# Four gate tiles leave the filling of the attention rounds and become two more Winograd column pairs

## The chip, the cores and the metric

One NeuronCore of a Trainium2 chip runs the whole program. The metric is the device time of one execution in microseconds (us). TensorE does the matrix products (PE in the profile; PEld its weight loads), VectorE is DVE, ScalarE ACT, GpSimd POOL, and SyncE (SP) issues nearly all DMAs.

## The reference

One decoder block over a sequence of 1024 tokens with width 1024, all float32, reduced here to the parts that the change touches:

```python
h = rms_norm(x, ln1_g)
proj = h @ w_in + b_in                  # 1024 x 6400
rq, rk, rv, rg, aq, ak, av, gate_a, gate_b = jnp.split(proj, SPLIT_IDX, axis=-1)
ry = head_group_norm(retention_chunkwise(rotary(rq), rotary(rk), rv), ret_norm_g)
branch_a = (silu(rg) * ry) @ w_ret_out
ay = sliding_window_sink_attention(rotary(aq), rotary(ak), av, attn_sinks)   # 16 heads of 64, window 128
branch_b = ay @ w_attn_out
merged = sigmoid(gate_a) * branch_a + sigmoid(gate_b) * branch_b             # both gates: 1024 columns of proj
x = x + merged @ w_out
x = x + (silu(h2 @ w_gate) * (h2 @ w_up)) @ w_down                           # h2 = rms_norm(x, ln2_g)
out = rms_norm(x, lnf_g)
```

gate_a and gate_b together are 2048 columns of the projection, 16 tiles of 128 columns, numbered 0 to 15 here (0 to 7 are gate_a).

## The kernel before

Every float32 operand of a product is split into a high and a low part (ScalarE casts the high part, VectorE subtracts to get the low one), and a product is three matmuls: high by high, high by low, low by high. A matmul has 128 rows of weights and streams 512 columns.

**Two ways to a column of the projection.** A *direct* tile of 128 columns costs 2 halves of the sequence x 8 blocks of the contraction x 3 = 48 matmuls (`mm_g`, lines 172 to 182). A *column pair* of 256 columns goes through a Winograd scheme of seven products P1 to P7 over half-size blocks, each 4 x 3 = 12 matmuls, so 84 for what costs 96 directly (`wproduct`, line 1018); for it POOL and DVE make sums of blocks. Before, eleven column pairs hold retention's q, k and swish gate and the gate tiles 0 to 5; the tiles 6 to 15 are direct.

**The attention stage.** It works through 32 units, one for a query block of 128 tokens (8 of them) and a quad of heads (4). A loop over i makes rounds, and in round i three units are at work. In the order of the program: the probabilities of unit i-2 are transposed on PE (`u_transpose`, L616), cast by ACT (L618), their low part taken by DVE (L619) and masked (L624); the scores of unit i are made on PE (`u_scores`, L581); ACT exponentiates unit i-1 (L604), and DVE normalises it (L607, L608); ACT and DVE copy out the scores of unit i and take their minimum (L590, L591, L593; L596 where the unit is the first of its quad); then comes the *filling*, and last the value products of unit i-2 on PE (`u_values`, L635). There is one pair of PSUM banks for scores, so the scores of unit i+1 wait until L591 has read those of unit i. The block is recorded under `in_order`: each of the five engines takes its instructions in just this order.

**The filling** is a list of items, run in steps of three matmuls: the projections of the q quads 1 to 3 (32 steps each, with rotary rotation behind them) and the direct gate tiles (16 steps each). Quad 0 and 20 steps are done ahead of round 0. `early` and `late` say how many steps the first `turn` rounds and the rest take. `prep` (L451 and L452 for a quad, L472 and L473 for a gate tile) splits the weights of the next item, from a slab of 512 KB which `load` has fetched into one of two buffers; the next loads (L442, L467) can start when both engines have read the old ones.

**The rotation** of half a quad is three tasks, one a round, at the end of the round's work on DVE: three operations (L514), three more, and two low parts (L533) after two casts on ACT (L530). The third also has SP store four tiles of 256 KB to `q_d` (L521); a round later SP reads them back in the layout for the scores (L526). The evicted halves (L492) use three rotating buffers of the tag `rab`, and the two `st` tiles have one buffer each, so an eviction or a first task waits for stores that still read the old tile.

After the filling come the products for retention's v (L861, DVE prepares sums of blocks for them), then the column pairs, the branch products, the output projection and the feed-forward part.

Of the kernel before, what the change touches and what calls it, by code (L numbers as in the profile page):

```python
# [20 lines left out]
NB = S // P  # L21
# [10 lines left out]
C_RQ, C_RK, C_RV, C_RG, C_AQ, C_AK, C_AV, C_GA, C_GB = (  # L32
    0, 512, 1024, 2048, 3072, 4096, 4224, 4352, 5376)
# [7 lines left out]
def hybrid_block(ctx: ExitStack, tc: tile.TileContext, x, ln1_g, w_in, b_in, ret_norm_g, w_ret_out,  # L41
# [74 lines left out]
    @contextmanager  # L116
    def in_order(*engines):

        traced = nc.cur_bb.bb.instructions
        last = traced[-1]  # L120
        yield
        start = next(k for k in reversed(range(len(traced))) if traced[k] is last) + 1
        prev = {}
        for i in traced[start:]:
            if i.engine in engines:
                if i.engine in prev:
                    tc.add_manual_dep(i, prev[i.engine],
                                      mybir.DependencyInfo(mybir.DependencyClass.NoSync, mybir.DependencyReason.DATA),
                                      reason="in_order")
                prev[i.engine] = i.name  # L130
# [194 lines left out]
    with tc.tile_pool(name="gt", bufs=1, side="right") as gt, tc.tile_pool(name="w1", bufs=1) as w1:  # L325
# [242 lines left out]
        def u_sink(u):  # L568
            g, b, nk, Bt, jb, qc = geo(u)
            scs[u] = (w1.tile([P, 4, 132], F32, tag="sc", bufs=3, name=f"sc{g}{b}"),  # L570
                      tiny.tile([P, 4], F32, tag="nm", name=f"nm{g}{b}"), tiny.tile([P, 4], F32, tag="den", name=f"den{g}{b}"))
            nc.gpsimd.tensor_copy(scs[u][0][:, :, P:P + 1], nsink[:, 4 * g:4 * g + 4].rearrange("p (j o) -> p j o", o=1))

        def u_scores(u):
            g, b, nk, Bt, jb, qc = geo(u)
            kv = g // 2
            k0 = (b - 1) * P if b > 0 else 0
            pt = sps[u] = spool[1].tile([P, 4, 2 * P], F32, tag="s4", name=f"s{g}{b}")
            for j in range(4):
                for z in range(2):  # L580
                    nc.tensor.matmul(pt[:, j, 0:nk], Bt[:, jb + j, qc], kst[:, kv, z, k0:k0 + nk], start=(z == 0),  # L581
                                     stop=(z == 1))

        def u_min(u):
            g, b, nk, Bt, jb, qc = geo(u)
            mk = amask[:, 0:P]
            pt = sps.pop(u)
            sc, nm, den = scs[u]
            if b > 0:
                nc.scalar.copy(sc[:, :, 0:P], pt[:, :, P:2 * P])  # L590
                nc.vector.copy_predicated(sc[:, :, 0:P], mk.bitcast(U32).rearrange("p (o s) -> p o s", o=1)  # L591
                                          .to_broadcast([P, 4, P]), pt[:, :, 0:P])
                nc.vector.tensor_reduce(out=nm, in_=sc[:, :, 0:P + 1], op=ALU.min, axis=mybir.AxisListType.X)  # L593
                return
            for j in range(4):
                nc.vector.tensor_tensor_reduce(out=sc[:, j, 0:P], in0=pt[:, j, 0:P], in1=mk, scale=1.0,  # L596
                                               scalar=nsink[:, 4 * g + j:4 * g + j + 1], op0=ALU.add, op1=ALU.min,
                                               accum_out=nm[:, j:j + 1])

        def u_exp(u):  # L600
            g, b, nk, Bt, jb, qc = geo(u)
            sc, nm, den = scs[u]
            for j in range(4):
                nc.scalar.activation(sc[:, j, 0:P + 1], sc[:, j, 0:P + 1], AF.Exp, scale=-1.0, bias=nm[:, j:j + 1],  # L604
                                     accum_out=den[:, j:j + 1])
            rd = tiny.tile([P, 4], F32, tag="rd", name=f"rd{g}{b}")
            nc.vector.reciprocal(rd, den)  # L607
            nc.vector.tensor_tensor(out=sc[:, :, 0:P], in0=sc[:, :, 0:P],  # L608
                                    in1=rd.rearrange("p (j o) -> p j o", o=1).to_broadcast([P, 4, P]), op=ALU.mult)

        def u_transpose(u):
            g, b, nk, Bt, jb, qc = geo(u)
            sc = scs.pop(u)[0]
            pt = ps("t", 2, f"pT{g}{b}")
            for j in range(4):
                nc.tensor.transpose(pt[:, j * P:(j + 1) * P], sc[:, j, 0:P], ident)  # L616
            p = w1.tile([P, 2, 512], F32R, tag="p", bufs=1, name=f"p{g}{b}")
            tie(acts, nc.scalar.copy(p[:, 0], pt))  # L618
            tie(vecs, nc.vector.tensor_tensor(out=p[:, 1], in0=pt, in1=f32(p[:, 0]), op=ALU.subtract))  # L619
            phs[u] = [(vev[:, b // 2], p)]  # L620
            if b > 0:
                mk = amask[:, P:2 * P].rearrange("p (o s) -> p o s", o=1).to_broadcast([P, 8, P])
                q = w1.tile([P, 2, 512], F32R, tag="q", bufs=1, name=f"q{g}{b}")
                nc.vector.scalar_tensor_tensor(out=q.rearrange("p z (j q) -> p (z j) q", j=4), in0=mk,  # L624
                                               scalar=float(b % 2 - 1), op0=ALU.add,
                                               in1=f32(p).rearrange("p z (j q) -> p (z j) q", j=4), op1=ALU.mult)
                phs[u].append((vdf[:, b - 1], q))
# [19 lines left out]
                nc.sync.dma_start(tb_d[n, :, half * 512:half * 512 + 512], t)  # L647
                yield

        order = list(range(6, 16))  # L650
        items = [QuadQ(0), QuadQ(1)] + [Gate(n) for n in order[0:2]] + [QuadQ(2)] + [Gate(n) for n in order[2:4]]
        items += [QuadQ(3)] + [Gate(n) for n in order[4:]]
        loaded = [0, 0]

        asked = [it for it in items for _ in range(it.raws)]
# [12 lines left out]
        def filling(n):  # L668
            it = items[n]
            while len(it.w) < it.size:  # L670
                prep(it)
            at = 23 if it.size == 2 else 4 if n + 1 < len(items) and items[n + 1].size == 2 else 0
            for k, _ in enumerate(it.products()):
                if k == at and n + 1 < len(items):
                    prep(items[n + 1])
                yield
# [6 lines left out]
        fl = Fill([filling(n) for n in range(1, len(items))])  # L683
        NU = 4 * NB
        fl.step(20)
        early, late, turn = 140, 68, 21
        with in_order(nc.tensor.engine, nc.sync.engine, nc.scalar.engine, nc.vector.engine, nc.gpsimd.engine):
            u_sink(0)
            for i in range(NU + 2):
                if i % NB == 0 and 0 < i < NU:  # L690
                    fl.until((1, 4, 7)[i // NB - 1])
                if i > 1:
                    u_transpose(i - 2)
                if i < NU:
                    u_scores(i)
                if 0 < i <= NU:
                    u_exp(i - 1)
                if i < NU:
                    u_min(i)
                while reads:  # L700
                    reads.pop(0)()
                on_act, on_dve, on_sp = task()
                do(on_act)
                if i + 1 < NU:
                    u_sink(i + 1)
                n, i0, m = (early, 0, turn) if i < turn else (late, turn, NU + 2 - turn)
                fl.step((i - i0 + 1) * n // m - (i - i0) * n // m)
                do(on_dve)
                do(on_sp)
                if i > 1:  # L710
                    u_values(i - 2)
                if 2 * NB + 4 <= i < 3 * NB + 4 and i % 2 == 0:
                    if i == 2 * NB + 4:
                        wv = act.tile([P, 16, 512], F32, tag="B", name="wv")
                    for q in ((1, 3, 0, 2)[i // 2 - NB - 2],):
                        nc.sync.dma_start(wv[:, 4 * q:4 * q + 4, :],
                                          w_in[(q // 2) * 512:(q // 2) * 512 + 512, C_RV + (q % 2) * 512:
                                               C_RV + (q % 2) * 512 + 512].rearrange("(k p) n -> p k n", p=P))
                if 3 * NB < i < NU and i % 2:

                    k = (i - 3 * NB) // 2
                    nc.vector.tensor_tensor(out=wv[:, 4 + k, :], in0=wv[:, 12 + k, :], in1=wv[:, 4 + k, :],
                                            op=ALU.subtract)
            fl.rest()
# [46 lines left out]
        return [kq.tile([P] + shape, F32, tag=t, name=f"{name}{t}") for t in ("kT", "qT")]  # L771

    cols = [c for h in range(RH) for c in ((C_RK, C_RQ, C_RK + 256, C_RQ + 256)[h], C_RG + 256 * h)]
    cols += [C_GA + 256, C_GA + 512, C_GA]
    NW = len(cols)

    with tc.tile_pool(name="rvp", bufs=1) as rvp:
# [528 lines left out]
    fl = Fill([bb_g(n) for n in range(8)])  # L1306
# [51 lines left out]
    with tc.tile_pool(name="w3", bufs=1) as w3:  # L1358
# [52 lines left out]
        late = in_order(nc.vector.engine, nc.scalar.engine)  # L1411
# [448 lines left out]
    early, kept = [], []  # L1860
# [268 lines left out]
```

## Time and profile before

| | |
|---|---|
| median of 3 runs | 1550.93 us (1550.89 to 1553.74) |
| profiled execution | 1553.45 us, span 1551.7 us, granted clock 0.997 |
| PE busy | 1539.0 us (99%), 7311 matmuls |
| DVE, ACT, POOL busy | 1026.2, 689.4, 406.4 us |
| attention rounds, scores of unit 0 to end of filling | about 78 to 318 us |
| column pairs | 400.2 to 605.6 us |

PE is busy nearly all of the span, so what counts is how many matmuls there are, how far apart they start, and where PE waits. A matmul of 512 columns is shown as lasting 0.39 us, but they overlap; the distance from one start to the next is their price. Where an engine takes its work in a fixed order, its own start-to-start distances are used in the same way.

### The profile page before, as it was taken

Reading aid. Unit: us, or ns where it says so; the run is one execution under the profiler, and the core shown is the slowest. Engines: PE = TensorE matmul, PEld = TensorE weight load, DVE = VectorE, ACT = ScalarE, POOL = GpSimd, SP = SyncE. Lnnn points to the kernel's source line nnn. Section 1 sums busy time; section 2 is a strip of 40 time slices with the busy share of each in tenths; the row PEclk is TensorE's granted clock in tenths of the full one; section 3 lists DMA queues with packets and bytes.
Section 4 is the critical chain, followed back from the end, with each engine's and each line's share of the span. In section 5 each row is a group of like instructions: output and inputs, shape, how many; then the busy total and the mean of one; then the engine's idle time right before and its main releaser. Section 6 shows DMA issues by size and latency. Waiting matters only on the chain.

```text
span 1551.7 us, 20401 instructions
## 1 busy us (share of the span) xinstructions
PE 1539.0 (99%) x7311; PEld 1284.6 (83%) x7311; DVE 1026.2 (66%) x1566; ACT 689.4 (44%) x1360; POOL 406.4 (26%) x356
## 2 busy tenths in 40 slices
PE   9999999999999999999999999999999999999998
PEld 8888887888888888888888888888888888888886
DVE  7587878697487774887457788444444444678656
ACT  6356656533334454544223465333333333344445
POOL 2011111100354430100111125655555555100001
PEclk9999999999999999999999999999999999999999
DMA  6654638402867756654556203333333333863233
GB/s 229 186 167 141 201 131 262 144 34 72 225 186 224 218 194 230 212 191 140 188 176 239 102 1 109 116 108 102 102 102 102 102 102 102 315 234 95 90 110 120
DMA packets 159025, 236.86 MB, mean 153 GB/s; under 512 B 10602, under 2 KB 82092, under 8 KB 158668
## 3 DMA queue, kind: packets, MB, share of 16 engines
q1 hardware_dynamic: 156316, 227.04, 45.6%
q0 software_dynamic: 2560, 8.39, 1.4%
q8 instruction: 57, 0.93, 0.3%
q14 instruction: 44, 0.36, 0.1%
q10 hardware_dynamic: 48, 0.13, 0.0%
HBM read 156.62 MB, written 74.19 MB: 149 GB/s over the span
## 4 chain that ended last, share of the span: by engine, by line
PE 92%; DMA 3%; DVE 2%; issue 1%; ACT 1%; SPq 0%; POOL 0%; POOLq 0%; DVEq 0%; ACTq 0%
PE fA L1753 15%; PE fB L1753 8%; PE dA L2055 7%; PE wA L1018 6%; PE dxP L2055 6%; PE fC L1753 4%; PE wB L1018 3%; PE va L861 3%; PE wo L1587 3%; PE acc_g L178 2%; PE acc_g L179 2%; PE acc_g L180 2%; PE woP L1587 2%; PE vP L861 2%; PE acc_ba L179 2%; PE acc_ba L180 2%
## 5 line engine op out<-in xcount | busy, mean ns | idle before, releaser
L2055 PE MATMUL dA<-dwP,daP 128*128 128x512 f32 x528 | 120.6, 389 | 0.0
L2055 PEld LDWEIGHTS dA<-dwP,daP 128*128 128x128 f32 x528 | 99.0, 188 | 20.8 <-DVE dwP L154 0.2
L2055 PE MATMUL dxP<-dwP,daP 128*128 128x512 f32 x396 | 90.2, 389 | 0.0
L2055 PEld LDWEIGHTS dxP<-dwP,daP 128*128 128x128 f32 x396 | 74.3, 188 | 15.4
L1828 POOL TENSOR_TENSOR xf<-xf 128x512 f32<-128x512 f32 x40 | 63.2, 1580 | 30.5 <-issue 28.9
L639 POOL DMA_DIRECT2D xy_d<-xy x32 | 23.1, 721 | 179.3 <-ACT xy L638 90.2
L178 PE MATMUL acc_g<-h,wh_g 128*128 128x512 f32 x160 | 63.8, 399 | 0.0
L179 PE MATMUL acc_g<-h,wh_g 128*128 128x512 f32 x160 | 63.3, 396 | 0.0
L180 PE MATMUL acc_g<-h,wl_g 128*128 128x512 f32 x160 | 63.0, 394 | 0.0
L1759 POOL TENSOR_TENSOR xf<-xf 128x512 f32<-128x512 f32 x33 | 47.3, 1434 | 58.8 <-ACT xf L1761 26.9
L1960 POOL TENSOR_TENSOR rs_f<-tot,mhalf 128x1 f32<-128x1 f32 x8 | 4.8, 606 | 205.4 <-DVE tot L1957 205.4
L154 DVE TENSOR_TENSOR dwP<-wd,dwP 128x512 fp32r<-128x512 f32 x77 | 52.8, 686 | 5.1 <-ACT dwP L151 5.1
L151 ACT CAST dwP<-wd 128x512 fp32r<-128x512 f32 x77 | 47.4, 616 | 9.4 <-PE dA L2055 6.8
L178 PE MATMUL acc_bb<-ay,wh_bb 128*128 128x512 f32 x128 | 51.0, 400 | 0.0
L730 POOL TENSOR_TENSOR wr_f<-wr_f 128x512 f32<-128x512 f32 x20 | 30.6, 1531 | 77.2 <-DVE t_8P L154 8.6
L151 ACT CAST daP<-daP 128x512 fp32r<-128x512 f32 x42 | 26.0, 622 | 54.8 <-PE dxP L2055 26.7
L180 PE MATMUL acc_bb<-ay,wl_bb 128*128 128x512 f32 x128 | 50.3, 393 | 0.0
L604 ACT ACTIVATE sc<-sc,nm 128x129 f32<-128x129 f32 x128 | 50.2, 403 | 0.2
L179 PE MATMUL acc_bb<-ay,wh_bb 128*128 128x512 f32 x128 | 50.2, 392 | 0.0
L178 PE MATMUL aq<-h,wh_aq 128*128 128x512 f32 x128 | 50.1, 391 | 0.0
L179 PE MATMUL aq<-h,wh_aq 128*128 128x512 f32 x128 | 50.0, 391 | 0.0
L178 PE MATMUL acc_ba<-yg,wh_ba 128*128 128x512 f32 x128 | 49.9, 390 | 0.0
(850 smaller groups left out, 4288.1 us busy)
## 6 DMA issues: line engine op xcount, KB each, us to landing
act_d<-xf SPq DMA_DIRECT2D x77, 256.0 KB, 2.1
daP<-act_d SPq DMA_DIRECT2D x21, 512.0 KB, 3.5
q<-q_d SPq DMA_DIRECT2D x32, 256.0 KB, 6.3
xy_d<-xy POOLq DMA_DIRECT2D x32, 256.0 KB, 3.3
wr_daP<-act_d SPq DMA_DIRECT2D x14, 512.0 KB, 6.5
wd<-in_w_ffn_down SPq DMA_DIRECT2D x6, 1024.0 KB
wr_wp<-in_w_in SPq DMA_DIRECT2D x11, 512.0 KB, 4.2
wp<-in_w_in SPq DMA_DIRECT2D x11, 512.0 KB
```

The costliest lines, as they stand in the source:

```text
L151: nc.scalar.copy(hi, raw)
L154: return nc.vector.tensor_tensor(out=lo, in0=raw, in1=f32(hi), op=ALU.subtract)
L178: nc.tensor.matmul(pt, hi[:, k, :], xh, start=(k == 0), stop=False)
L179: nc.tensor.matmul(pt, hi[:, k, :], xl, start=False, stop=False)
L180: nc.tensor.matmul(pt, lo[:, k, :], xh, start=False, stop=(k == 7))
L604: nc.scalar.activation(sc[:, j, 0:P + 1], sc[:, j, 0:P + 1], AF.Exp, scale=-1.0, bias=nm[:, j:j + 1], accum_out=den[:, j:j + 1])
L861: nc.tensor.matmul(vbanks[pr][tt], x_[:, c], w[:, u, :], start=(fresh and k + z == 0), stop=(k == 3 and z == 2), skip_group_check=not fresh)
L1018: nc.tensor.matmul(pt, o[:, w, k, :], v, start=(first and k + z == 0), stop=(k == 3 and z == 2), skip_group_check=not first)
L1587: nc.tensor.matmul(bank, v[:, q + u, k, c], w[y][:, k % 2, :], start=(first and z == 0), stop=(last and z == 2), skip_group_check=not tracked)
L1753: nc.tensor.matmul(pt, o[:, w, k, :], v, start=(first and n == 0), stop=(n == 11), skip_group_check=not first)
L1828: nc.gpsimd.tensor_tensor(out=o, in0=a, in1=b, op=op)
L2055: nc.tensor.matmul(banks[tt], a[:, u, c], w[:, v, :], start=(fresh and f + z == 0), stop=(f == NP - 1 and z == 2), skip_group_check=not fresh)
```

## The change

Gate tiles 6 to 9 leave the filling, and two column pairs are added at the end of the pairs' list: `C_GA + 768` (tiles 6 and 7) and `C_GB` (tiles 8 and 9). The filling is now quad 1, quad 2, gate 10, quad 3 and gates 11 to 15: 192 steps where there were 256. The rounds 0 to 20 take 99 steps where they took 140 (4.7 a round for 6.7), the others 45 for 68 (3.5 for 5.2). The thresholds in `fl.until` follow.

```diff
@@ the filling of the attention
-        order = list(range(6, 16))
-        items = [QuadQ(0), QuadQ(1)] + [Gate(n) for n in order[0:2]] + [QuadQ(2)] + [Gate(n) for n in order[2:4]]
-        items += [QuadQ(3)] + [Gate(n) for n in order[4:]]
+        order = list(range(10, 16))
+        items = [QuadQ(0), QuadQ(1), QuadQ(2), Gate(order[0]), QuadQ(3)] + [Gate(n) for n in order[1:]]
@@
-        early, late, turn = 140, 68, 21
+        early, late, turn = 99, 45, 21
@@
-                    fl.until((1, 4, 7)[i // NB - 1])
+                    fl.until((1, 2, 4)[i // NB - 1])
@@ the column pairs
-    cols += [C_GA + 256, C_GA + 512, C_GA]
+    cols += [C_GA + 256, C_GA + 512, C_GA, C_GA + 768, C_GB]
```

SP's queue at the start of the rounds, before. `q_d` is the rotated q on its way through memory, `wr_g` and `wr_aq` are raw weights of a gate tile and of a quad, the last four rows are the stores of quad 1's first half:

```order
L526 DMA q_675<-q_d 32x4x512 x4
L467 DMA wr_g_840<-in_w_in 128x8x128
L467 DMA wr_g_842<-in_w_in 128x8x128
L442 DMA wr_aq_950<-in_w_in 128x4x256
L442 DMA wr_aq_1013<-in_w_in 128x4x256
L647 DMA tb_d<-tb_1072 128x512
L521 DMA q_d<-q_869 128x512
L521 DMA q_d<-st_960 128x512
L521 DMA q_d<-st_959 128x512
L521 DMA q_d<-q_896 128x512
```

The same place now:

```order
L526 DMA q_675<-q_d 32x4x512 x4
L442 DMA wr_aq_840<-in_w_in 128x4x256
L442 DMA wr_aq_842<-in_w_in 128x4x256
L467 DMA wr_g_1047<-in_w_in 128x8x128
L442 DMA wr_aq_1049<-in_w_in 128x4x256
L521 DMA q_d<-q_869 128x512
L521 DMA q_d<-st_953 128x512
L521 DMA q_d<-st_952 128x512
L521 DMA q_d<-q_896 128x512
```

Quad 2 needs both raw buffers until its second split in round 2, so the two loads ahead of the four stores (`wr_g_1047`, `wr_aq_1049`) wait for that split now; before, the buffers were those of gates 6 and 7, split in rounds 0 and 1.

ACT in round 5, before (from the exponentials to the next round's cast; `q_944` is the first part of quad 1's second half, L530 the two casts of its third task):

```order
L604 ACTIVATE sc_1122,den_1124<-sc_1122,nm_1123 128x129 x4
L590 COPY sc_1187<-s_1243 128x4x128
L530 ACTIVATE q_944<-st_1146 128x512
L530 ACTIVATE st_1145<-q_1120 128x512
L646 ACTIVATE tb_1277<-acc_g_0_1200,bhalf 128x512
L638 COPY xy_1304<-pv_1299 128x512
L618 CAST p_1312<-pT_1307 128x512
```

The same place now:

```order
L604 ACTIVATE sc_1106,den_1108<-sc_1106,nm_1107 128x129 x4
L590 COPY sc_1164<-s_1207 128x4x128
L530 ACTIVATE q_944<-st_1123 128x512
L530 ACTIVATE st_1122<-q_1104 128x512
L492 ACTIVATE q_1247<-aq_1176,bcol 128x512
L638 COPY xy_1260<-pv_1255 128x512
L618 CAST p_1268<-pT_1263 128x512
```

Where a gate tile's tanh stood (L646), there is now the eviction of quad 2's second part, `q_1247`. It takes the buffer of `q_944`, whose low part and store belong to the third task of the same round.

DVE in round 21 and at the start of round 22 now (the second task of quad 3's second half, with 9 filling matmuls on PE in that round; before, this task stood in round 23, with 15):

```order
L619 TENSOR_TENSOR p_2222<-pT_2217,p_2222 128x512
L624 SCALAR_TENSOR_TENSOR q_2225<-amask,p_2222 128x1024
L607 RECIPROCAL rd_2240<-den_2110 128x4
L608 TENSOR_TENSOR sc_2108<-sc_2108,rd_2240 128x4x128
L591 COPY_PREDICATED sc_2183<-amask,s_2227 128x4x128
L593 TENSOR_REDUCE nm_2184<-sc_2183 128x4
L514 TENSOR_TENSOR q_2000<-q_2000,atab 128x512
L514 TENSOR_TENSOR q_2181<-q_2181,atab 128x512
L514 TENSOR_TENSOR q_2181<-q_2181,q_2000 128x512
L619 TENSOR_TENSOR p_2279<-pT_2274,p_2279 128x512
L624 SCALAR_TENSOR_TENSOR q_2282<-amask,p_2279 128x1024
```

The six operations of a round and the rotation's tasks are the same instructions as before; only the number of matmuls that PE has beside them is smaller.

## The prediction

> **What bounds the kernel now.** I read the page's busy shares first, then the attention's rounds in order of time on PE and on DVE, then its windows.
>
> ```profile
> PE 1539.0 (99%) x7311; PEld 1284.6 (83%) x7311; DVE 1026.2 (66%) x1566; ACT 689.4 (44%) x1360; POOL 406.4 (26%) x356
> ```
>
> PE is busy 99% of the span; the page itself says that matmul ends are modelled, so the price of a matmul is taken from starts. Round to round, by the transposes that begin each:
>
> ```profile
> 171.03 0.60 PE L616 MATMUL pT<-ident,sc 128*128 128x128 f32 x4
> 178.14 0.60 PE L616 MATMUL pT<-ident,sc 128*128 128x128 f32 x4
> 184.55 0.60 PE L616 MATMUL pT<-ident,sc 128*128 128x128 f32 x4
> ```
>
> The first of these rounds lasts 7.11 us with 21 filling matmuls, the second 6.41 with 18. So three matmuls cost 0.70, one 0.23, and the rest of a round is 7.11 - 21 x 0.23 = 2.28 us of PE work; I use 2.27. A matmul of the column pairs is a little cheaper: eleven pairs, 924 matmuls, lie between these two starts, 205.35 us or 0.222 each:
>
> ```profile
> 400.23 2.88 PE L1018 MATMUL wA<-h,w0P 128*128 128x512 f32 x12
> ...
> 605.58 1.03 PE L1158 MATMUL kTT<-ident,r 128*128 128x128 f32 x8
> ```
>
> DVE in a round and a half, in order of time (start, duration; the next start says what an operation takes of the engine):
>
> ```profile
> 169.88 1.28 DVE L514 TENSOR_TENSOR q<-q,atab 128x512 f32<-128x512 f32 x2
> 171.20 0.69 DVE L514 TENSOR_TENSOR q<-q,q 128x512 f32<-128x512 f32 x1
> 172.34 0.69 DVE L619 TENSOR_TENSOR p<-pT,p 128x512 fp32r<-128x512 f32 x1 [0.45 <-ACT p L618]
> 173.07 1.23 DVE L624 SCALAR_TENSOR_TENSOR q<-amask,p 128x1024 fp32r<-128x1024 f32 x1
> 174.21 0.17 DVE L607 RECIPROCAL rd<-den 128x4 f32<-128x4 f32 x1
> 174.42 0.69 DVE L608 TENSOR_TENSOR sc<-sc,rd 128x512 f32<-128x512 f32 x1
> 175.03 0.74 DVE L591 COPY_PREDICATED sc<-amask,s 128x512 f32<-128x512 uint32 x1
> 175.87 0.69 DVE L593 TENSOR_REDUCE nm<-sc 128x4 f32<-128x516 f32 x1
> 176.48 1.28 DVE L452 TENSOR_TENSOR wl_aq<-wr_aq,wh_aq 128x512 fp32r<-128x512 f32 x2
> 177.68 0.69 DVE L533 TENSOR_TENSOR st<-st,q 128x512 fp32r<-128x512 f32 x1
> 178.28 0.68 DVE L533 TENSOR_TENSOR q<-q,st 128x512 fp32r<-128x512 f32 x1
> ```
>
> From 172.34 to 176.48 it does a round's six operations in 4.1 us. A rotation task of three operations takes 1.9 (169.88, 171.20 and 0.6 more), a pair of low parts 1.2 (177.68, 178.28), a split of weights 1.2 (176.48 to 177.68). The low part of p begins 1.31 us after the transposes when DVE is free (171.03 to 172.34). A round with a task needs 5.3 to 6.0 us of DVE, with a split 1.2 more. A window of nearly six rounds:
>
> ```profile
> 140.00:180.00 40.00, 40.00 (x213) 34.11 (x212) 35.84 (x55) 26.04 (x77) 5.23 (x12) 1.00 0.43 141
> ```
>
> DVE is busy 35.84 of 40 us and PE never idle: PE sets the pace, with a tenth of DVE to spare. One place in the rounds is different. The starts of rounds 3 and 33:
>
> ```profile
> 96.19 0.60 PE L616 MATMUL pT<-ident,sc 128*128 128x128 f32 x4
> ...
> 293.79 0.60 PE L616 MATMUL pT<-ident,sc 128*128 128x128 f32 x4
> ```
>
> The waits of PE in between, at rounds 23 and 24:
>
> ```profile
> 236.60 0.73 PE L635 MATMUL pv<-q,vdf 128*128 128x512 f32 x2 [0.47 <-DVE q L624]
> 237.51 0.63 PE L616 MATMUL pT<-ident,sc 128*128 128x128 f32 x4 [0.18 <-DVE sc L608]
> 239.67 1.94 PE L581 MATMUL s<-kst,q 128*128 128x128 f32 x8 [1.53 <-DMA q<-q_d]
> ```
>
> And the windows there (the last three columns are granted clock, DMA share and GB/s):
>
> ```profile
> 236.00:240.00 4.00, 1.82 (x9) 1.08 (x8) 3.86 (x7) 2.40 (x9) 0.00 (x0) 0.89 0.84 280
> 240.00:244.00 4.00, 4.00 (x14) 3.50 (x14) 3.90 (x11) 2.62 (x8) 1.64 (x2) 0.50 0.73 283
> 244.00:248.00 4.00, 4.00 (x15) 3.10 (x14) 2.93 (x7) 0.66 (x1) 0.00 (x0) 0.76 0.33 98
> ```
>
> Rounds 3 to 32 last 197.6 us. PE's own work in them is 546 x 0.23 + 30 x 2.27, less 2.7 for the units that have no earlier block and for the missing scores of round 32: 191.0. The other 6.6 us are lost around 236: PE waits for a mask, a normalisation and 1.53 us for q that SP reads back, and then runs at half speed. The three windows show 0.89, 0.50 and 0.76 of the clock: (0.11 + 0.50 + 0.24) x 4 = 3.4 us lost by the clock alone.
>
> **The change part by part.** *Matmuls.* Out go 4 x 48 = 192 at 0.23, 44.2 us; in come 2 x 84 = 168 at 0.222, 37.3 us in a stage where 924 of them took 205.35 us with hardly a gap. I take the 37.3 whole, bounds 37 and 39. Of the 192, 18 lie in rounds 0 to 2, 168 in rounds 3 to 32, 6 in the tail. The added splits, sums and tanh calls lie beside PE as those of the other pairs do.
>
> *Rounds 3 to 32.* PE's own work falls from 191.0 to 378 x 0.23 + 65.4 = 152.3 us. DVE keeps its work, less one wait: 30 x 4.1, less 5.9 for first units and the end, plus 36.2 of tasks, splits and sums of the v weights, about 153.5 together. The two are equal now, where DVE had 158 in 197.6, and they are unevenly spread. I went through the rounds one by one: the low part of p starts 1.31 after the transposes or when DVE is done with the round before, whichever is later; the value products wait until the mask is made (1.9 after that start, 172.34 to 174.21), the next scores until L591 has ended (3.4 after, 175.03 + 0.73). Grouped:
>
> | rounds | PE alone | DVE alone | with the waits |
> |---|---|---|---|
> | 3-8 | 32.8 | 35.5 | 36.8 |
> | 9 | 5.7 | 4.1 | 6.3 |
> | 10-12 | 16.0 | 18.6 | 17.3 |
> | 13-16 | 22.2 | 16.1 | 23.0 |
> | 17-24 | 41.1 | 45.0 | 45.8 |
> | 25-32 | 36.0 | 34.3 | 38.5 |
> | sum | 153.8 | 153.6 | 167.7 |
>
> (The sums by group differ from 152.3 by rounding of the special rounds.) The worst are rounds 21 and 22: 9 matmuls and 2.3 are 4.3 us of PE against 6.0 of DVE. So 167.7 instead of 197.6: 29.9 saved where the matmuls alone promise 38.6 plus the 6.6.
>
> *The start.* Before, PE's scores of unit 1 and its first transposes, ACT's split of gate 6, DVE's part of that split and its first normalisation:
>
> ```profile
> 83.13 1.12 PE L581 MATMUL s<-kst,q 128*128 128x256 f32 x8
> 89.33 0.63 PE L616 MATMUL pT<-ident,sc 128*128 128x128 f32 x4 [0.30 <-ACT wh_g L472]
> ```
>
> ```profile
> 84.13 1.05 ACT L472 CAST wh_g<-wr_g 128x1024 fp32r<-128x1024 f32 x1 [1.47 <-DMA wr_g<-in_w_in]
> ```
>
> ```profile
> 85.21 1.23 DVE L473 TENSOR_TENSOR wl_g<-wr_g,wh_g 128x1024 fp32r<-128x1024 f32 x1 [4.89 <-ACT wh_g L472]
> 88.49 0.69 DVE L608 TENSOR_TENSOR sc<-sc,rd 128x512 f32<-128x512 f32 x1
> ```
>
> PE waited 0.30 us for the first transposes, because the raw weights of gate 6 came at 84.13, then cast, exponentials and DVE's chain (split, three-operation task, normalisation) followed. The loads now at that place are as large, so they come as late. Two half casts let DVE start its split some 0.5 earlier: transposes at about 88.8. But PE, with 18 - 6 and 21 - 6 matmuls, is there at 83.13 - 1.4 + 1.03 + 15 x 0.23 = 86.2. It waits 2.6 us. Round 3 then starts near 94.4 for 96.19: 1.8 saved, not 4.1.
>
> *Stores.* Two places of SP's queue and of `rab` cost more than that. Around 227, before, on SP, ACT and DVE:
>
> ```profile
> 226.49 0.37 SPq L467 DMA_DIRECT2D wr_g<-in_w_in  x1
> 226.91 0.72 SPq L521 DMA_DIRECT2D q_d<-q  x1
> ```
>
> ```profile
> 231.83 0.69 ACT L492 ACTIVATE q<-aq,bcol 128x512 f32<-128x512 f32 x1 [3.98 <-DVE nm L593]
> ```
>
> ```profile
> 232.67 1.30 DVE L514 TENSOR_TENSOR st<-q,atab 128x512 f32<-128x512 f32 x2 [0.90 <-DMA q_d<-st]
> ```
>
> A store of q issued at 226.91 behind a 512 KB load let ACT's eviction go only at 231.83, after 4.9 us, and DVE's next task waited 0.90. The row of ACT names a reduction of DVE that ended at about that time; but the eviction writes the buffer that this store reads, and the view of DMA issues in this window gives 5.0 us to its landing, 231.9:
>
> ```profile
> q_d<-q SPq DMA_DIRECT2D x2, 256.0 KB, 5.0
> ```
>
> In the change the four stores of round 2 stand behind two loads that wait for the split in that same round (about 96), 2 MB in all; at the 280 GB/s of the window at 236 they have landed some 7 us later, near 103. DVE is ready for the next task at 101.6: 1.6 us, and ACT's eviction waits as long, behind it the cast of the next round, within the same 1.6. In round 5 ACT evicts `q_1247` into the buffer that DVE's last task of that round reads; behind it wait the copy of the values and the next cast. That task begins 7.4 us after the transposes (DVE late by 3.2, then 4.1), so the cast ends 9.8 after, where DVE could go on at 8.6: 1.3 us. Round 20 repeats the first place with one load: 0.7. Together 3.6, bounds 0 (DVE late anyway for another reason) and 8 (twice as long, as two loads are twice the one).
>
> *The lost stall.* Quad 3's first half is now rotated by round 19 and read five rounds before use instead of three, so the wait for q at 239.67 goes; it is in the 197.6 already.
>
> *The clock.* PE had 1.82 us of work in the 4 us from 236 and was halved. The 2.6 us wait at the start leaves about as little in 4 us, so I reckon one halving there, 3.4 us, half of it hidden since PE waits for DVE in round 3 anyway: 1.7, bounds 0 and 3.4. The Trainium skill, TensorE: Matmul & The Clock Gate, Part 1, has the clock halved after an idle window of about 3.4 us, in free-running windows; the trace does not agree that the whole window must be idle. By that rule no wait here is long enough, and the sum would be 1.7 less.
>
> *Tail.* 6 matmuls less: 1.4.
>
> Sum: -1.8 - 29.9 - 1.4 + 37.3 + 3.6 + 1.7 = +9.5 on the profiled execution's own 1553.45: 1563.0. The runs of before lie from 2.6 below that execution to 0.3 above it; I take 1562, own range 1554 to 1570.
>
> **The rivals.** *PE stays the bound*: DVE's overhang is always caught up before PE needs it. For it: PE is never idle beside 35.84 of 40 us of DVE. Against: the groups where DVE alone is longer, and the 0.47 and 0.18 us that PE waited for DVE at 236 with 15 matmuls a round. Then rounds 3 to 32 take 153.8: -1.8 - 43.8 - 1.4 + 37.3 = -9.7, 1543.7. This one ends on the other side, and decides if waits in the rounds stay under 4 us. *DVE sets the pace without a gap*: each group takes the longer of its two columns, 163.0, stores and clock cost nothing: -1.8 - 34.6 - 1.4 + 37.3 = -0.5, 1553, no change. It needs PE and DVE to hand over without the fixed 1.3 and 1.9 us between them. *The clock is halved again and again*: rounds 3 to 8 and 17 to 24 have PE waits in nearly every round. Against: PE still works two thirds of round 21, for 45% at 236. Two or three halvings more: 1570; five: 1580.
>
> **How the numbers follow.** Forecast 0.62, PE the bound 0.15, DVE without a gap 0.12, repeated halving 0.11. A change below 0.2%, 3.1 us, cannot be told from none: faster is under 1547.8, slower over 1554.0. Faster: 0.15 and a little of the second rival, 0.17. Same: 0.09 of it and 0.05 of the forecast's lower end, 0.14. Slower: 0.69. The range, 1546 to 1573, leaves out about half of the first rival's cases and of the last one's.
>
> **What would show it.** Right: DVE busy over 95% in rounds 3 to 8 and 17 to 24, PE idle about 14 us in the rounds, named for L624, L608 and L591; a wait of 2 to 3 us before the first transposes; ACT waiting for a store at L492 in rounds 3 and 5; no wait of scores for q; thirteen pairs at 18.7 us each. Wrong: PE idle under 4 us in the rounds (first rival), a clock near 0.9 over the rounds (last), or pairs above 20 us, which no part of the sum has.

## The result and the profile after

| | before | after |
|---|---|---|
| median | 1551.34 us (1550.89 to 1553.74) | 1564.92 us (1563.53 to 1566.51) |
| profiled execution | 1553.45 us, span 1551.7 us | 1565.66 us, span 1563.9 us |
| PE busy | 1539.0 us, 7311 matmuls | 1540.7 us, 7287 matmuls |

The change makes the kernel slower: the ratio of the times is 1.0083, with an interval of 1.0070 to 1.0097. (The medians differ by 13.6 us, the profiled executions, which the parts below are read from, by 12.2.) PE has 24 matmuls less to do and its share of the span is still shown as 99%. The page's busy row of the changed kernel:

```profile
PE 1540.7 (99%) x7287; PEld 1275.8 (82%) x7287; DVE 1032.6 (66%) x1582; ACT 698.3 (45%) x1376; POOL 421.7 (27%) x364
```

So the loss is not read from that row. It is read from starts, as in the prediction: round 3's and round 33's transposes, the first product of the column pairs, and the first instruction of PE behind the pairs.

```profile
94.77 0.60 PE L616 MATMUL pT<-ident,sc 128*128 128x128 f32 x4
...
267.28 0.63 PE L616 MATMUL pT<-ident,sc 128*128 128x128 f32 x4 [0.17 <-DVE sc L608]
...
366.91 2.88 PE L1017 MATMUL wC<-h,w0P 128*128 128x512 f32 x12
...
617.48 1.03 PE L1157 MATMUL kTT<-ident,r 128*128 128x128 f32 x8
```

And the first product of the pairs before, which the prediction had not quoted; so the pairs began at 394.8 there and not at 400.2, as the table of the profile before has it:

```profile
394.79 2.88 PE L1018 MATMUL wC<-h,w0P 128*128 128x512 f32 x12
```

With 96.19, 293.79 and 605.58 from the prediction's rows this divides the spans into five parts:

| part | before | after | difference | forecast |
|---|---|---|---|---|
| to round 3 | 96.19 | 94.77 | -1.4 | -1.8 |
| rounds 3 to 32 | 197.60 | 172.51 | -25.1 | -24.6 (-29.9, stores +3.6, clock +1.7) |
| tail and retention's v | 101.00 | 99.63 | -1.4 | -1.4 |
| column pairs | 210.79 | 250.57 | +39.8 | +37.3 |
| behind the pairs | 946.1 | 946.4 | +0.3 | 0 |
| sum | | | +12.2 | +9.5 |

The 168 matmuls that leave the rounds are 38.2 us at 0.2275 each, and the loss at 236 was 6.6 us more; 25.1 came. The groups of rounds in the windows view (length, then PE, PEld, DVE, ACT and POOL busy, clock, DMA share, GB/s):

```profile
94.77:135.01 40.24, 36.61 (x182) 27.53 (x180) 35.55 (x55) 24.45 (x76) 7.48 (x12) 1.00 0.60 190
135.01:141.40 6.39, 6.03 (x32) 4.97 (x33) 6.08 (x16) 3.06 (x11) 1.33 (x2) 1.00 0.67 213
141.40:158.60 17.20, 16.79 (x90) 13.55 (x88) 14.60 (x24) 14.13 (x42) 3.26 (x6) 1.00 0.33 104
158.60:181.84 23.24, 23.07 (x122) 18.94 (x122) 19.37 (x36) 13.55 (x46) 4.16 (x8) 1.00 0.61 194
181.84:228.46 46.62, 43.50 (x223) 33.61 (x222) 42.85 (x65) 32.66 (x99) 9.35 (x16) 1.00 0.59 187
228.46:267.28 38.82, 38.09 (x203) 30.90 (x203) 33.99 (x58) 28.07 (x93) 7.26 (x14) 1.00 0.53 189
94.77:267.28 172.51, 164.09 (x846) 129.50 (x844) 152.42 (x251) 115.91 (x364) 32.85 (x58) 1.00 0.56 182
```

The lengths are those of the forecast's table with its stores: 40.2 for 36.8 + 2.9 (rounds 3 to 8), 6.4 for 6.3, 17.2 for 17.3, 23.2 for 23.0, 46.6 for 45.8 + 0.7 (rounds 17 to 24), 38.8 for 38.5. The waits of PE from 80 to 270 us (in total, times, the longest):

```profile
PE pT L616 <- DVE sc L608: 5.2, 14, 2.9
PE pv L635 <- DVE q L624: 3.7, 8, 0.8
PE pv L635 <- DVE p L619: 1.6, 2, 1.0
PE s L581 <- DVE nm L596: 0.7, 2, 0.4
```

All name DVE. L608 and L624 were forecast, and L596 stands for the forecast's L591 in the first unit of a quad. L619, the low part of p itself, was not: its two waits are in rounds 4 and 21, where DVE is late for a store (below). The first row holds the wait at the start:

```profile
89.28 0.63 PE L616 MATMUL pT<-ident,sc 128*128 128x128 f32 x4 [2.91 <-DVE sc L608]
```

How DVE's lateness goes from round to round, in round 5, whose transposes start at 109.18:

```profile
110.38 1.28 DVE L514 TENSOR_TENSOR q<-q,atab 128x512 f32<-128x512 f32 x2
111.70 0.69 DVE L514 TENSOR_TENSOR q<-q,q 128x512 f32<-128x512 f32 x1
112.31 0.68 DVE L619 TENSOR_TENSOR p<-pT,p 128x512 fp32r<-128x512 f32 x1
```

DVE goes from the rotation's task straight to the low part of p, without a pause, 3.1 us after the transposes instead of the 1.31 that it takes when DVE is free.

But the rows of waits add up to 11.2 us, 2.9 of them at the start, while rounds 3 to 32 last 20 us longer than their matmuls cost (152.3). The windows above show 8.4 us of idle time (172.51 - 164.09). Two ends of rounds, one with waits and one without, show where the rest is:

```profile
108.27 0.73 PE L635 MATMUL pv<-q,vdf 128*128 128x512 f32 x2 [0.76 <-DVE q L624]
109.18 0.63 PE L616 MATMUL pT<-ident,sc 128*128 128x128 f32 x4 [0.18 <-DVE sc L608]
...
140.93 0.63 PE L635 MATMUL pv<-q,vdf 128*128 128x512 f32 x2
141.40 0.60 PE L616 MATMUL pT<-ident,sc 128*128 128x128 f32 x4
```

From the value products to the transposes it is 0.91 us with waits and 0.47 without, though only 0.18 of that is called idle: matmuls that a steady stream overlaps stand one behind the other after a wait, and the page says that their ends are modelled. So the idle rows give less than half of what waiting costs here, and only start-to-start distances give all of it.

The two places of the stores, in rounds 3 and 20 of the program (PE feels them in rounds 4 and 21). SP's queue, ACT and DVE of the changed kernel:

```profile
95.98 0.37 SPq L467 DMA_DIRECT2D wr_g<-in_w_in  x1
96.59 0.39 SPq L442 DMA_DIRECT2D wr_aq<-in_w_in  x1
97.02 0.49 SPq L521 DMA_DIRECT2D q_d<-q  x1
```

```profile
103.54 0.69 ACT L492 ACTIVATE q<-aq,bcol 128x512 f32<-128x512 f32 x1 [5.48 <-DMA q_d<-q]
...
117.20 0.69 ACT L492 ACTIVATE q<-aq,bcol 128x512 f32<-128x512 f32 x1 [3.51 <-DVE st L533]
...
206.30 0.69 ACT L492 ACTIVATE q<-aq,bcol 128x512 f32<-128x512 f32 x1 [4.26 <-DMA q_d<-q]
```

```profile
104.34 1.29 DVE L514 TENSOR_TENSOR st<-q,atab 128x512 f32<-128x512 f32 x2 [2.46 <-DMA q_d<-st]
...
206.95 1.37 DVE L514 TENSOR_TENSOR st<-q,atab 128x512 f32<-128x512 f32 x2 [0.62 <-DMA q_d<-st]
```

The store of 97.02 stands behind two loads. ACT waits 5.48 us for it, DVE 2.46 for the next one, and 4.26 and 0.62 us in round 20. The second row of ACT is the other cost that was forecast: the eviction that waits for a low part of the same round.

### The profile page after: what moved, and what is told of

Read it like the earlier page. It is cut to its first block, busy times and chain, and to the rows that moved or that the text cites. A ratio compares the mean times of both kernels' runs of the same rounds, so it can differ in the third digit from the quotient of the medians.

```text
span 1563.9 us, 20425 instructions
## 1 busy us (share of the span) xinstructions
PE 1540.7 (99%) x7287; PEld 1275.8 (82%) x7287; DVE 1032.6 (66%) x1582; ACT 698.3 (45%) x1376; POOL 421.7 (27%) x364
## 4 chain that ended last, share of the span: by engine, by line
PE 86%; DVE 8%; DMA 2%; issue 2%; ACT 1%; POOL 0%; SPq 0%; POOLq 0%; DVEq 0%; ACTq 0%
PE fA L1752 15%; PE wA L1017 8%; PE fB L1752 8%; PE dA L2054 7%; PE dxP L2054 6%; PE wB L1017 4%; PE fC L1752 4%; PE va L860 3%; PE wo L1586 3%; PE woP L1586 2%; PE wC L1017 2%; PE vP L860 2%; PE acc_ba L178 2%; PE acc_ba L179 2%; PE acc_ba L180 2%
## 5 line engine op out<-in xcount | busy, mean ns | idle before, releaser
L729 POOL TENSOR_TENSOR wr_wp<-wr_wp 128x512 f32<-128x512 f32 x13 | 20.5, 1579 | 138.7 <-DVE w0P L154 92.5
L180 PE MATMUL aq<-h,wl_aq 128*128 128x512 f32 x128 | 49.9, 389 | 0.0
L180 PE MATMUL acc_ba<-yg,wl_ba 128*128 128x512 f32 x128 | 49.8, 389 | 0.0
```

What stands on the lines that cost most here:

```text
L180: nc.tensor.matmul(pt, lo[:, k, :], xh, start=False, stop=(k == 7))
L729: nc.gpsimd.tensor_tensor(out=o, in0=a, in1=b, op=ALU.subtract)
```

## The experiments

Times of one group were taken beside the kernel before on the same chip; its median there is given. These medians lie between 1551.3 and 1552.1, so a difference between groups of about 1 us says little. Where a diff changes the order of the filling, the thresholds in `fl.until` follow. "Rounds" is the stretch from round 2's transposes to round 33's, 178.0 us in the changed kernel (89.28 to 267.28) and 204.5 before.

### The thin rounds without the pairs

The kernel before, with the change's filling order and density, and gates 6 to 9 at the end of the filling, so in the tail.

```diff
-        items = [QuadQ(0), QuadQ(1)] + [Gate(n) for n in order[0:2]] + [QuadQ(2)] + [Gate(n) for n in order[2:4]]
-        items += [QuadQ(3)] + [Gate(n) for n in order[4:]]
+        items = [QuadQ(0), QuadQ(1), QuadQ(2), Gate(order[0]), QuadQ(3)] + [Gate(n) for n in order[1:]]
-        early, late, turn = 140, 68, 21
+        early, late, turn = 99, 45, 21
```

> The kernel before (ten gate tiles in the filling, eleven column pairs) with the changed kernel's order of items and its 99 and 45 steps, so that its rounds are those of the change and the 192 matmuls of gates 6 to 9 come in the tail, where nothing waits. Theory (the thin rounds wait for DVE): rounds 2 to 32 last 178 us as in the changed kernel, and the only difference to it is 192 direct matmuls at 0.2275 (43.7) for two pairs (39.8): 1564.9 + 3.9 = 1569. Rival (the added pairs and their loads cost the time, the rounds do not): 1551 or, with the wait for q at 236 gone, 1545.

Measured: 1568.88 us beside 1552.08 of the kernel before, ratio 1.0106 (1.0091 to 1.0122). Rounds 178.3. The theory's 1569 is met and the rival falls: the same matmuls, only fewer of them a round, cost this kernel 17 us with not one pair added.

### More matmuls in the rounds

```diff
-        early, late, turn = 99, 45, 21
+        early, late, turn = 116, 54, 21
```

> The changed kernel with 116 and 54 steps for 99 and 45: the rounds get 15 to 18 and 12 matmuls, the tail 21 for 96. Nothing is added or left out. Theory (PE waits for DVE in the rounds, so matmuls put there are nearly free): rounds 2 to 32 go from 178.0 to 180.0 though 69 matmuls (15.7 us) come in, the tail loses 75 (17.1): 15 less, 1550. Rival (a wait of fixed length in each round, whatever PE does there): matmuls cost the same in both places, 1563.5. Rival (the tail covers work of DVE and ACT ahead of retention's v): part of the 15 comes back as a wait of the first products of v.

Measured: 1565.49 beside 1552.08, ratio 1.0086 (1.0071 to 1.0101), no gain. The rounds did what the theory says: 180.25 us for 180.0, so 69 matmuls more cost 2.2 us there. But the gain is given back right behind them, as the third theory had it, and in full. PE's first products for retention's v in this kernel:

```profile
283.16 7.97 PE L860 MATMUL va<-vP,h 128*128 128x512 f32 x24 [6.52 <-DVE vP L154]
...
296.46 7.90 PE L860 MATMUL va<-vP,h 128*128 128x512 f32 x23 [5.33 <-DVE vP L154]
```

DVE at that place, the first sum of blocks for v:

```profile
278.88 2.36 DVE L791 TENSOR_TENSOR vacc<-h 128x1024 f32<-128x1024 f32 x2 [5.59 <-DMA xy_d<-xy]
```

These sums can start only when the last value copies have landed (5.59 us of waiting on `xy_d`), and PE then waits for them twice, 11.9 us in all, with the clock at 0.50 behind each wait (283 to 287 and 296 to 300 us). The waiting and about 5 us at the slow clock are the 17 us that the shorter tail had saved. The tail of 96 matmuls, 21.8 us, hides that: 21 of them (4.8 us) and 11.9 of waiting make 16.7 that it has to be long. Little of it is spare.

### DVE's work left out

```diff
-            tasks.append(([], [lambda: tt(a, a, sn, ALU.mult), lambda: tt(b, b, cs, ALU.mult),
-                               lambda: tt(b, b, a, ALU.add)], []))
+            tasks.append(([], [lambda: tt(a, a, sn, ALU.mult), lambda: tt(b, b, cs, ALU.mult),
+                               lambda: tt(b, b, a, ALU.add)] if g == 0 else [], []))
@@
-                          [lambda: low(s2, s2, a), lambda: low(b, b, s1)], [store]))
+                          [lambda: low(s2, s2, a), lambda: low(b, b, s1)] if g == 0 else [], [store]))
```

> The changed kernel without part of the rotation of quads 1 to 3: the three operations of each second task and the two low parts of each third are left out (six of each, 18.6 us of DVE), the casts and stores stay. Theory (DVE sets the pace): going through the rounds one by one, 10.8 us less, 1554; the rest of the 18.6 only makes DVE idle. Rival (ACT, the score banks or stores set the pace): 1565. Rival (PE is the bound): 1565 too, with PE idle little in both.

Measured: 1559.91 beside 1552.08, ratio 1.0051 (1.0034 to 1.0068): 5 us less than the change, not 11. Round by round most of the 30 rounds came within 0.1 us of the working. Four did not: 4 and 21 were 2.5 and 2.0 us over it, 26 and 27 together 4.1. What ACT waited for from 196 to 235 us:

```profile
ACT xy L638 <- DMA xy_d<-xy: 10.2, 3, 3.7
ACT q L492 <- DMA q_d<-q: 2.9, 1, 2.9
```

So with DVE's work gone, the stores of q decide in rounds 4 and 21, and in 25 to 27 copies of the values (L638), which wait for the stores of older copies while the DMA engines are full (share 1.05 and 400 GB/s from 224 to 230 us, with `wv` on its way). I then took away the first of the two, loads standing ahead of stores:

```diff
+        hold = []
         def load_ahead():
-            while asked and loaded[1] < 2:
+            while asked and loaded[1] < 2 and not hold:
@@ in the loop over rounds
+                hold.extend(on_sp)
                 fl.step((i - i0 + 1) * n // m - (i - i0) * n // m)
                 do(on_dve)
                 do(on_sp)
+                hold.clear()
+                load_ahead()
```

> The changed kernel with the same operations of the rotation left out as before (the second task's three and the third's two low parts, quads 1 to 3), and the raw weight loads of a round behind its stores. Theory: the 10.8 us that leaving DVE's work out should have saved came down to 5 because stores behind loads (4.5 us in rounds 4 and 21) and copies that waited for stores of the values beside the wv loads (4.1 us in rounds 26 and 27, clock included) took DVE's place. Without the first: 1560 - 4.5 = 1555.5; if the second goes too as the times shift, 1551.5. Rival (something else in the rounds bounds them): 1560 again.

Measured: 1557.16 (1553.40 to 1558.64) beside 1551.27, ratio 1.0033 (1.0021 to 1.0045). The profiled execution took 1558.64; its rounds last 170.2 us for 162.5 by the working. Rounds 4 and 21 are 0.3 and 0.0 under it: this part is settled. Rounds 25 to 27 are 5.8 over, and ACT's waits there, from 210 to 235 us, name the same copies:

```profile
ACT xy L638 <- DMA xy_d<-xy: 11.2, 3, 5.3
```

The theory's 1551.5 to 1555.5 is met by the fastest executions and missed by the median. The stretch ahead of those copies shows DVE's part by itself: rounds 3 to 24 last 119.9 us here and 128.8 in the next experiment, which has the loads behind the stores too but all of DVE's work, and PE alone would need about 117. So DVE is the first bound of the thin rounds, and stores are close behind it. That these copies cost nothing of the kind in the changed kernel itself (1.6 us of such waiting from 80 to 270, and its rounds 25 to 28 within 0.2 us of the working) is shown; why they meet the `wv` loads only when the rounds come earlier was not tested apart.

### Loads behind the stores

The edit above alone, in its first form (every round holds its loads).

> The changed kernel with the raw weight loads of a round issued on SP behind that round's stores of q, not ahead. Theory (the stores of rounds 2 and 19 land late because loads of 1 and 0.5 MB are served first, and ACT and DVE wait for them in the rounds behind): rounds 3 and 4 lose 1.8 and round 21 0.75 against the working with DVE alone, and both go: 2.5 less, 1562.4. Rival (DVE is late there for its own work): 1565. Rival (the loads, now later, delay the next split): 1566 or more.

Measured: 1561.18 beside 1552.08, ratio 1.0061 (1.0046 to 1.0076), 3.7 less than the change. Rounds 174.5: rounds 3 and 4 together are 3.6 us shorter than with the change, round 21 0.8, and round 2 is 1.6 longer in this execution, where the wait at the start was 4.32 and the clock stood at 0.50 behind it. Together that is 2.9 us. The waits were the stores', not DVE's own, and cost about the 2.5 that I had worked out for them; that they cost more, as the 3.7 of the medians would have it, is not shown, since those are of two groups.

### The order alone

```diff
-        items = [QuadQ(0), QuadQ(1)] + [Gate(n) for n in order[0:2]] + [QuadQ(2)] + [Gate(n) for n in order[2:4]]
-        items += [QuadQ(3)] + [Gate(n) for n in order[4:]]
+        items = [QuadQ(0), QuadQ(1), Gate(order[0]), QuadQ(2), Gate(order[1]), QuadQ(3)] + [Gate(n) for n in order[2:]]
```

> The kernel before with the order of its filling alone changed: quad 1, gate 6, quad 2, gate 7, quad 3, gates 8 to 15, the same steps a round, all gates and pairs as before. Theory: quad 3 is rotated and read back rounds earlier, so the wait for q, the two behind it and the slow clock at 236 go (6.6 us) and PE sets the pace in every round: rounds 2 to 32 go from 204.5 to 198, in all 1545.5. Rival (the waits at 236 move to another place, as loads and stores meet there too): 1549 to 1552. By this the loss at 236 would be no part of what the fewer matmuls of the change could save.

Measured: 1547.53 beside 1551.27, ratio 0.9975 (0.9964 to 0.9986). That is 3.7 us less than before, for the 6 expected. In the profiles it is 5.9 (spans 1545.8 and 1551.7), since the profiled execution of before is among its longer ones. Rounds 199.0 for 204.5; PE waits once in them, by the view of waits from 80 to 290 us:

```profile
PE pT L616 <- DVE sc L608: 0.2, 1, 0.2
```

The loss at 236 was a matter of the order, as the prediction took it, and it could be had without any of the rest.

### Half of the change

Gates 6 and 7 go to one pair, 8 and 9 stay (120 and 56 steps); then the same with loads behind stores.

```diff
-        items = [QuadQ(0), QuadQ(1), QuadQ(2), Gate(order[0]), QuadQ(3)] + [Gate(n) for n in order[1:]]
+        items = [QuadQ(0), QuadQ(1), Gate(order[0]), QuadQ(2), Gate(order[1]), QuadQ(3)] + [Gate(n) for n in order[2:]]
-        early, late, turn = 99, 45, 21
+        early, late, turn = 120, 56, 21
-    cols += [C_GA + 256, C_GA + 512, C_GA, C_GA + 768, C_GB]
+    cols += [C_GA + 256, C_GA + 512, C_GA, C_GA + 768]
```

> Half of the change: gates 6 and 7 go to one more column pair, gates 8 and 9 stay in the filling; 120 and 56 steps, quads one gate apart. Theory (DVE sets the pace where a round has under about 15 to 18 matmuls): rounds 2 to 32 take 180 by the working round by round and about 3 for stores, tail 0.7 less, start 0.7 less, pair 19.5: 1548.5, so 3 more than the kernel before with its quads early (1545.5), and 16 less than the change. Rival (each pair costs the same): half way between 1545.5 and 1565, 1555. Rival (PE stays the bound with one pair): 1545.5 - 21.8 + 19.5 = 1543.

> As the one with one more pair, and in a round that stores rotated q the raw weight loads stand behind the stores on SP. Theory: what the stores cost there goes, 2 to 3 us: 1546. Rival (PE has matmuls enough to cover late stores with 15 to 18 a round): the same as without, 1548.5.

Measured: 1549.42 and 1547.69 beside 1551.27, ratios 0.9992 (0.9983 to 1.0001) and 0.9979 (0.9970 to 0.9987). Rounds 181.9 and 180.7. Half of the change costs 2 us over the order alone, not half of 17: with 15 and 18 matmuls PE sets the pace, and only rounds 21 to 23, with 12 beside a task of the rotation, and 24 wait. With the loads behind the stores nothing is left of the 2 us, and nothing is gained either. So the loss does not go with the number of pairs but sets in where a round's matmuls fall below DVE's work.

### Splits on POOL

```diff
-                tie(vecs, nc.vector.tensor_tensor(out=lo, in0=self.raw, in1=f32(hi), op=ALU.subtract))
+                (nc.gpsimd if slow else nc.vector).tensor_tensor(out=lo, in0=self.raw, in1=f32(hi), op=ALU.subtract)
```

(the same for the quads' splits, `slow` being set inside the rounds; the raw weight loads stand behind the stores, as above)

> The changed kernel with the low parts of the weight splits in the rounds (two operations of 128x512 a quad half, one of 128x1024 a gate, 1.2 us of DVE each time, eleven times) on POOL instead of DVE, and the raw weight loads of a round behind its stores. Nothing is left out. Theory (the rounds wait for DVE): by the working round by round 178.0 goes to 166.6, in all 1553.5; up to 4 more if copies of the values meet late stores in rounds 25 to 27 as where the rotation was thinned, 1557.5. Rival (POOL takes 1.6 us for 512 columns where DVE takes 0.6, so that weights come late): 1561 or more.

> The same with one more pair for two (gates 6 and 7 moved, 120 and 56 steps, loads behind stores). Theory: rounds 2 to 32 go from 180.7 to 179 at most, since PE sets the pace nearly everywhere: 1546, against 1547.7 with the splits on DVE. Rival (POOL's operations delay the copies of the values or the weights): 1548 or more.

Measured: 1562.18 and 1547.61 beside 1551.65, ratios 1.0071 (1.0058 to 1.0083) and 0.9972 (0.9963 to 0.9981). Neither gains over its partner with the splits on DVE (1561.18 and 1547.69); rounds 2 to 32 take 175.6 us for the 166.6 of the theory, and 181.3 for 179. The rival's number came, but not by its mechanism: no matmul waits for weights. POOL and DVE in round 10 of the two-pair kernel with splits on POOL:

```profile
142.10 2.99 POOL L452 TENSOR_TENSOR wl_aq<-wr_aq,wh_aq 128x512 fp32r<-128x512 f32 x2 [2.37 <-ACT wh_aq L451]
```

```profile
142.75 2.89 DVE L514 TENSOR_TENSOR st<-q,atab 128x512 f32<-128x512 f32 x2
```

The same two multiplications of DVE where the split is its own, in the kernel with loads behind stores:

```profile
146.30 1.29 DVE L514 TENSOR_TENSOR st<-q,atab 128x512 f32<-128x512 f32 x2
```

1.29 us became 2.89: the second of them ends 0.55 us, its own length, after POOL's two operations (145.09). DVE pays for the split by standing still, 1.6 us for the 1.2 that it was spared. It is not the only place: summed over rounds 2 to 32 of the two-pair kernels, DVE is spared 10.2 us of splits, and its operations of the rotation (L514 and L533) and the mask (L624) take 8.6 us longer. The Trainium skill, SBUF — State Buffer, Who interferes with whom, says that a DVE instruction with two SBUF inputs contends with a GpSimd instruction that reads SBUF, and that the contention is an exclusive lock; the trace agrees.

### A denser half

The half of the change with loads behind stores, and the steps moved so that every round with a rotation task has 15 or 18 matmuls.

```diff
-        early, late, turn = 120, 56, 21
+        early, late, turn = 130, 46, 23
```

> One more pair, loads behind stores, and 130 steps in rounds 0 to 22 and 46 behind (for 120 in rounds 0 to 20 and 56), so that all rounds with rotation tasks have 15 or 18 matmuls. Theory: the 1.6 us that rounds 21 to 24 wait for DVE go, and 3 matmuls move: rounds 2 to 32 from 180.7 to 179.7, 1546.5. Rival (rounds 23 to 32, now thinner, wait instead): 1547.7, as before.

Measured: 1546.65 (1544.91 to 1547.59) beside 1551.64, ratio 0.9964 (0.9951 to 0.9978). Rounds 179.0. One wait is left from 80 to 270 us, at the start:

```profile
PE pT L616 <- DVE sc L608: 0.6, 1, 0.6
```

This is the fastest median of the study, though 1547.53 of the order alone lies within its spread: no kernel with a pair added is shown to be faster than the one with the order alone.

## Why the prediction was right, and where it was off

- **Direction and size.** 1562 was forecast for 1564.92, in the own range of 1554 to 1570. The mechanism is the forecast's: DVE paces thin rounds. The kernel with thin rounds and no new pair shows by itself that the rounds lose the time (1568.88), the kernel with DVE's work left out and the loads behind the stores that it is DVE's work (rounds 3 to 24, 119.9 for 128.8), and the half change where it begins.
- **Rounds 3 to 32.** Working 167.7 + 3.6 + 1.7 = 173.0, measured 172.51. With the stores in their groups and without the clock, each group is within 0.6. The starts, the hand-over times and the order on each engine were enough for that; that the sum is within 0.5 is partly luck (see the clock).
- **Stores.** Right in place, a little small in size: 2.3 forecast for the stores behind loads (1.6 and 0.7), and moving the loads took 2.9 off rounds 2 to 4 and 21 and 3.7 off the median; 1.3 forecast for the eviction behind a low part of the same round, and rounds 6 and 7 are 1.2 over the working. Together 4 to 5 for 3.6, inside the bounds of 0 and 8.
- **Clock.** 1.7 forecast, nothing found in this profile: all windows of the rounds show 1.00. In the profile with thin rounds and no pair the halving did come at the same place, and its rounds last 178.3 against 178.0. So even then it costs 0.3, since PE has DVE and a store to wait for behind it. I had taken half of it as hidden, and nearly all of it was. The rounds last 4.8 us over the 167.7 of the working, for which the two terms had 3.6 + 1.7; that a clock term which did not come made up for stores that were too small is luck.
- **Column pairs.** This is the term that was too small, 37.3 with bounds of 37 and 39 for 39.8 measured: "eleven pairs, 924 matmuls, lie between these two starts". They do not: the first product of the pairs starts at 394.79, 24 matmuls earlier than the row I took. 900 matmuls in 205.35 are 0.228 each, not 0.222. A pair in which PE does not wait takes 19.04 us, 0.2267 a matmul, the two added ones among them. A direct matmul costs the same, where I had it a little dearer: the kernel with thin rounds and no new pair has 192 more of those in its tail, which is 43.5 us longer, 0.2266 each. So the two pairs themselves cost 38.1. The other 1.7 us are in pairs that were there before, the third and the sixth to eighth: four waits for DVE's split of block sums, where there was one before:

```profile
408.71 2.60 PE L1017 MATMUL wC<-h,w2P 128*128 128x512 f32 x10 [0.38 <-DVE w2P L154]
412.09 2.56 PE L1017 MATMUL wA<-s,w2P 128*128 128x512 f32 x10 [0.33 <-DVE w2P L154]
...
464.48 2.56 PE L1017 MATMUL wB<-s4h,w4P 128*128 128x512 f32 x10 [0.31 <-DVE w4P L154]
...
503.56 2.56 PE L1017 MATMUL wB<-s4h,w6P 128*128 128x512 f32 x10 [0.38 <-DVE w6P L154]
```

They are no price of the added pairs: thirteen pairs took 247.55 us, 13 x 19.04, in the kernel with more matmuls in the rounds, and 250.89 in the one with DVE's work left out and loads behind stores. What makes DVE late there in some of these executions was not tested.

- **Start.** 2.6 us of waiting forecast, 2.91 measured, round 3 at 94.77 for 94.4.
- **What would show it.** The waits, their lines, ACT's waits at L492 in rounds 3 and 5 (the first named for a store, the second for the low part ahead of it) and the missing wait for q were all there. "DVE busy over 95%" in rounds 3 to 8 and 17 to 24 was not: 35.55 of 40.24 (88%) and 42.85 of 46.62 (92%), since DVE itself waits for stores and casts in them. "PE idle about 14 us in the rounds" was 8.4, for the reason given at the waits above. The pairs take 19.3 us each for the 18.7 forecast.
- **The rivals.** *PE stays the bound* falls with the waits, but nearly holds for one pair. (Its time was about 1 us too high: in the table, 41.1 for PE alone in rounds 17 to 24 should be 40.2, since 96 x 0.23 + 8 x 2.27 is all there is. The forecast does not rest on that figure.) *DVE without a gap* (163.0 for the rounds) falls with 172.5. *Repeated halving* falls with the clock of 1.00.

## What to carry to other kernels

Work that is cheaper elsewhere may be what hides another engine: before taking matmuls out of a stretch, add up the other engines' work for it, round by round and in their order, and take out only down to that. Judge such a stretch by the distance from start to start, since idle rows showed under half of what the waiting cost. And test the parts of a bundled change one by one: here an earlier place for quad 3 in the order alone gave 0.25%, and the change, against that, lost more than four times as much.

## What the hardware showed that was not expected

- Moving DVE's subtractions to POOL freed next to nothing: two multiplications of DVE took 2.89 us beside POOL's split and 1.29 without.
- The same wait at the start halved the clock in one execution and not in the other. The changed kernel waited 2.91 us for its first transposes, and the windows behind show:

```profile
88.00:90.00 2.00, 0.72 (x5) 0.59 (x6) 1.86 (x5) 0.06 (x1) 0.00 (x0) 1.00 0.00 0
90.00:92.00 2.00, 2.00 (x13) 1.82 (x14) 1.97 (x4) 1.93 (x8) 0.19 (x1) 1.00 0.00 0
92.00:94.00 2.00, 2.00 (x10) 1.64 (x10) 1.97 (x5) 2.00 (x6) 0.00 (x0) 1.00 0.00 0
```

The kernel with thin rounds and no new pair waited 2.89 us:

```profile
88.00:90.00 2.00, 0.84 (x6) 0.71 (x7) 1.86 (x5) 0.17 (x1) 0.09 (x1) 1.00 0.00 0
90.00:92.00 2.00, 2.00 (x11) 1.81 (x11) 1.97 (x4) 1.93 (x9) 0.10 (x1) 0.63 0.00 0
92.00:94.00 2.00, 2.00 (x6) 1.52 (x6) 1.97 (x5) 1.66 (x5) 0.00 (x0) 0.52 0.00 0
```

At the same place 2.24 us were followed by 0.50 in the kernel with more matmuls in the rounds, and 2.88 by 1.00 in the one with DVE's work left out and loads behind stores, so the length of the wait does not decide alone. The Trainium skill, TensorE: Matmul & The Clock Gate, Part 1, has free-running windows of about 3.4 us, one of which must be idle before the clock is halved. That one of two equal waits is caught fits windows that run free; that a wait shorter than a window is caught at all does not fit a window that must be idle throughout. In the kernel with DVE's work left out, a wait of 1.34 us, with PE busy for 2.3 of the 4 us from 228 to 232, was followed by 0.50 of the clock:

```profile
231.27 1.08 PE L616 MATMUL pT<-ident,sc 128*128 128x128 f32 x4 [1.34 <-DVE sc L608]
```

```profile
230.00:232.00 2.00, 0.73 (x4) 0.76 (x5) 1.65 (x4) 0.65 (x3) 0.00 (x0) 0.81 0.49 195
232.00:234.00 2.00, 2.00 (x11) 2.00 (x10) 0.56 (x1) 0.03 (x1) 0.00 (x0) 0.50 0.06 25
```
